# Pair 7 of the second FFN's down projection as seven block products, with a second weight sum by DMA in three groups

## The chip, the cores and the metric

The kernel runs on one core of a Trainium2 chip. The metric is the device time of one execution in microseconds: 547.79 us is the median of three runs of the kernel before. The engines are named as the profile names them: PE (TensorE), DVE (VectorE), ACT (ScalarE), POOL (GpSimd) and SP (SyncE, which issues most transfers).

## The reference

One decoder layer on 256 tokens of width 1024, all in float32: a half-step SwiGLU FFN, a mixer of two attentions, a second half-step FFN, and a final norm.

```python
def swiglu(x, w_gate, w_up, w_down):
    return (jax.nn.silu(x @ w_gate) * (x @ w_up)) @ w_down

h = h + FFN_RES * swiglu(rms_norm(h, ffn1_norm[l]), ...)
h = h + hybrid_mixer(rms_norm(h, mix_norm[l]), ...)
h = h + FFN_RES * swiglu(rms_norm(h, ffn2_norm[l]), ffn2_w_gate[l], ffn2_w_up[l], ffn2_w_down[l])
return rms_norm(h, final_norm)
```

The change is in the last product of the second FFN, the down projection: 256 x 2816 hidden values by a 2816 x 1024 matrix.

## The kernel before, in words

**Tiles and precision.** All weights come as one stream of 376 tiles of 128 x 512 floats, two to a chunk of 512 KB. A product of float32 values is made of three matmuls (`mm3`, L381 to L383): each operand is split into a high part (float32r, the rounded value) and a low part (what is left), and high x high, high x low and low x high are added in PSUM. One such triple is called a unit. For each weight tile ACT writes the high part `wh` (L236) and DVE the low part `wl` (L237); in the products that follow a norm, L240 and L241 do the same with the norm's gain. The class `Weights` does this ahead of use: 12 buffers for `wh` and `wl`, `split` at most 11 tiles ahead in the down projection, SP's loads of chunks six buffers ahead. A chunk is loaded again when the tiles in it have been read.

**The down projection.** The hidden values are 22 blocks k of 128 (11 pairs, numbered 0 to 10), by two token blocks t and two column halves c. A plain pair has 4 weight tiles, each used for both t: 8 units. In the pairs of `SEVENS` the 2 x 2 x 2 block product is made by seven units instead of eight (the Strassen-Winograd form). They use seven weight tiles, each once: tiles s, s+2, s+3 as loaded and four sums T3 to T6 of them, and four sums of the hidden blocks (`cs`, L589 to L592, then split into `c` at L412 and L413). Four results go to the banks X, Y, Z and V (`dn_f2XY`, `dn_f2ZV`), the rest directly to the outputs' banks. `post` combines X, Y, Z and V after the last such pair and adds them to the residual `h` (L710 to L724, with L707).

**Who makes the weight sums.** T3 = tile s + tile s+1 is made by GpSimd's transfers (`given`): one loads tile s (L206), a second adds tile s+1 to it in the transfer (L208). They are issued 16 and 11 places ahead of the group. T4 = tile s+3 + tile s+1, T5 = tile s+3 + T3 and T6 = tile s+2 + T5 are made by DVE (`seventh`, L216), each just before a split.

**The rest of POOL's queue.** The hidden values are transposed by 16 small transfers for each two pairs (`exchange`, L537; `hm_f<-hs_f`). For the last three pairs (8, 9 and 10) POOL issues them, between the transfers of T; then ACT and DVE split the result (`hth_f`, `htl_f`). POOL issues in order, and a transfer that adds waits for its load to land.

**The tail.** In the second FFN `TAILS` leaves the last four blocks, pairs 9 and 10, to the end: eight weight tiles, used for one output half after the other. As an output half is done, DVE adds it to `h` (`residual`, L680) and the final norm of its row block goes on: a square on ACT (L418), sums and the reciprocal root on DVE and ACT, the product with the gain (`hg`), the result and its store. The last half (1,1) comes in two pieces of 256 columns (`dn_f2p`).

**What sets the order.** From the third block of the second FFN on, all engines run in the order in which the code records instructions (`manual_schedule`). A generator-based scheduler, `Weave`, ticks once a unit; delayed steps (`post` after 3 ticks, then one step a tick) are recorded between units, and `weave.flush()` ahead of the tail records all that is left.

Of the kernel before, what the change touches and what calls it, by code (L numbers as in the profile page):

```python
# [8 lines left out]
F32 = mybir.dt.float32  # L9
# [8 lines left out]
P = 128  # L18
T = 256
# [8 lines left out]
NEG = -1e30  # L28
CH = 2
N_TILES = 376  # L30
SEVENS = (0, 2, 4, 6), (0, 2, 3, 5, 6)
ADDED = 0,
W_IN = FB * KD + 2 * KF + 3 * len(SEVENS[0])
W_BR = W_IN + 10 * KD
W_OUT = W_BR + 16
# [2 lines left out]
WB = 12  # L38
# [22 lines left out]
AHEAD0 = 4  # L61
# [42 lines left out]
class Weave:  # L104


    def __init__(self):
        self.now = 0
        self.tasks = []
# [30 lines left out]

def _items():

    out, n = [], 0

    def plain(count):
        nonlocal n
        out.extend((n + i, None) for i in range(count))
        n += count

    for f in range(2):  # L150
        plain(FB * KD)
        for g in range(KF // 2):
            if g in SEVENS[f]:
                out.extend((n, j) for j in range(7))
                n += 4
            else:
                plain(4)
        if f == 0:
            plain(W_FFN2 - W_IN)
    assert n == N_TILES  # L160
    return out


class Weights:


    def __init__(self, nc, pool, early, sums, spare, stream, gain, bufs, ahead):
        self.early, self.sums, self.spare, self.items = early, sums, spare, _items()
        self.nc, self.pool, self.stream, self.gain = nc, pool, stream, gain
        self.bufs, self.ahead = bufs, ahead  # L170
        self.loaded = self.ready = self.freed = self.at = 0
        self.raw, self.parts, self.behind = {}, {}, {}
        self.made, self.ahead_of = {}, {}
        for i, (s, j) in enumerate(self.items):
            if j == 0:
                for step, lead in enumerate((AHEAD_LOAD, AHEAD_ADD)):
                    self.ahead_of.setdefault(i - lead, []).append((s, step))

    def load(self, n, tiles=0):

        n = min(n, N_TILES // CH)
        while self.loaded < n * CH + tiles:
            c, j = divmod(self.loaded, CH)
            if j == 0:
                nm = f"raw{c}"
                self.raw[c] = self.early(nm) if c < 12 else self.pool.tile([P, CH * 512], F32, name=nm, tag="raw", bufs=RAW)
            step = 1 if c < 3 else CH
            s = slice(j * 512, (j + step) * 512)
            if {0, 1} <= set(ADDED) and (c * CH, 0) in self.items:
                s = slice(0, 512)  # L190
            for piece in HALVES if self.loaded == 0 else (s,):
                self.nc.sync.dma_start(self.raw[c][:, piece], self.stream[c, :, piece])
            self.loaded += step
# [6 lines left out]

    def given(self, s, step):

        for n in ADDED:
            if step == 0:
                self.made[s, 3 + n] = self.spare(f"T{s}_{3 + n}")
                self.nc.gpsimd.dma_start(self.made[s, 3 + n], self.source(s + 3 * n))  # L206
            else:
                self.nc.gpsimd.dma_start(self.made[s, 3 + n], self.source(s + 1), accum_op=ALU.add)  # L208

    def seventh(self, s, j):  # L210

        if 0 < j < 4 and not (j == 1 and 1 in ADDED):
            a, b, o = ((3, 1, 4), (3, 3, 5), (2, 5, 6))[j - 1]
            self.made[s, o] = self.sums(f"T{s}_{o}")
            b = self.made[s, b] if j > 1 else self.tile(s + b)
            self.nc.vector.tensor_add(self.made[s, o], self.tile(s + a), b)  # L216
        raw = self.made.pop((s, j)) if j > 2 else self.tile(s + (0, 2, 3)[j])
        return raw, {1: s // CH, 3: s // CH + 1}.get(j)
# [50 lines left out]
def hybrid_layer_kernel(ctx, tc, x, xt, pos, g_final, bgate, wstream, out):  # L269
    nc = tc.nc  # L270
# [5 lines left out]
    wpool = ctx.enter_context(tc.tile_pool(name="wpool", bufs=1))  # L276
    work = ctx.enter_context(tc.tile_pool(name="work", bufs=1))
# [11 lines left out]
    def big(nm, dt=F32R):  # L289
        return work.tile([P, 1024], dt, name=nm, tag="big", bufs=20)  # L290
# [7 lines left out]
    def row512(nm):  # L298
        return work.tile([P, 512], F32, name=nm, tag="tok", bufs=4)

    def spare512(nm):
        return work.tile([P, 768], F32, name=nm, tag="r", bufs=4)[:, 0:512]

# [6 lines left out]
    def gain(i):  # L310
# [7 lines left out]
                return gk[:, n * KD + k:n * KD + k + 1]  # L318
        return None

    W = Weights(nc, wpool, lambda nm: big(nm, F32), row512, spare512, wstream, gain, WB, AHEAD0)

    xin = [big(f"xin{j}", F32) for j in range(2)]

    def load_x(queue, k0, k1):
        s = slice(k0 % 4 * T, k0 % 4 * T + (k1 - k0) * T)
        queue.dma_start(xin[k0 // 4][:, s], xt[:, 3 * KD + k0 * T:3 * KD + k1 * T])


    nc.scalar.dma_start(first, xt[:, 0:3 * KD + T])  # L330
    W.load(0, 1)
    nc.scalar.preload_act_table_set("silu_and_others")
    W.load(1)
    load_x(nc.sync, 1, 2)
    W.load(2)
    load_x(nc.sync, 2, 3)
    W.load(3)
    load_x(nc.sync, 3, 4)
    W.load(4)
    load_x(nc.sync, 4, 6)  # L340
    W.load(6)
    load_x(nc.sync, 6, 8)
# [21 lines left out]
    sums = consts.tile([P, 2 * P], F32R, name="sums")  # L364
# [190 lines left out]
    def ffn(base, xn, nm, on_half, lag, last=False):  # L555
# [3 lines left out]
        squares = {}  # L559
        sevens = SEVENS[1 if last else 0]  # L560

# [316 lines left out]
    def project(bi, evac):  # L878
        banks = {}
        for t, k in lagged(KD, KD if bi == 0 else 2):  # L880
            if k == 0:
                banks[t] = acc_bank(f"in{bi}_{t}")
            i = W_IN + bi * KD + k
            unit(banks[t], un[t].blk(k), W.get(i), k == 0, k == KD - 1)
            if t == 1:
                W.done(i)
            if k == KD - 1:
                evac(t, banks[t])
# [219 lines left out]

    gates = {}
    for gi in range(4):  # L1110
        bg = work.tile([P, 512], F32, name=f"bg{gi}", tag="bg", bufs=2)
        src = bgate[gi * 512:(gi + 1) * 512]
        with tc.issue_after(marks["rot"]):
            nc.gpsimd.dma_start(bg, bass.AP(tensor=src.tensor, offset=src.offset, ap=[[0, P], [1, 512]]))

        def evac_g(t, ps, gi=gi, bg=bg):
            if gi % 2 == 0:
                gates[gi // 2, t] = big(f"gate{gi}_{t}", F32)
            g = gates[gi // 2, t][:, gi % 2 * 512:gi % 2 * 512 + 512]
            nc.vector.scalar_tensor_tensor(g, ps, un[t].r, bg, op0=ALU.mult, op1=ALU.add)  # L1120

        project(6 + gi, evac_g)
# [57 lines left out]
    for c in range(2):  # L1180
        s = slice(c * 512, c * 512 + 512)
# [110 lines left out]
```

## Time and profile before

| what | us |
| --- | --- |
| median of three runs (547.63, 547.79, 549.13) | 547.79 |
| the profiled execution's own time | 547.91 |
| its span, first to last instruction | 546.1 |
| PE busy / DVE busy / ACT busy / POOL busy | 538.4 / 450.1 / 355.5 / 126.2 |
| the second down projection: first weight split on ACT, last matmul's end | 473.89, 539.66 |

The span lies 1.8 us under the time of the same execution. TensorE's granted clock is 0.998 of full speed on average. A matmul's row has 0.39 us but rows start 0.227 us apart, since matmuls overlap; rows of DVE overlap by some 0.08 us in the same way. So the pace of an engine is read from starts, not from durations. In a row of the timeline the number in brackets is the engine's idle time before it, with what ended it.

### The profile page before, as it was taken

What the parts mean: (1) busy time and instruction counts of PE and PEld (TensorE: products, weight loads), DVE (VectorE), ACT (ScalarE), POOL (GpSimd) and SP (SyncE); (2) the same over time, 40 slices, a digit from 0 to 9 for tenths busy, and PEclk for the clock granted to TensorE, in tenths of its full rate; (3) what the DMA queues carried; (4) which work ended last, traced back from release to release, by engine and by line L of the source; (5) the groups of instructions that cost most, each with busy time, mean ns of one, the idle gap of its engine ahead of it and who ended that gap; (6) DMA issues with size and microseconds to landing.
All of it is one profiled execution on the core that took longest, in us unless ns stands there. A gap on an engine that the chain in (4) does not pass through costs nothing.

```text
span 546.1 us, 8019 instructions
## 1 busy us (share of the span) xinstructions
PE 538.4 (99%) x2463; PEld 444.4 (81%) x2463; DVE 450.1 (82%) x806; ACT 355.5 (65%) x616; POOL 126.2 (23%) x243
## 2 busy tenths in 40 slices
PE   9999999999999999999999999999999999999995
PEld 6888888888888888888888888888888888888884
DVE  5797799889998766889888888876667887899995
ACT  5876556658773766677876775466566566667743
POOL 2430000035405826022022220384000000157000
PEclk9999999999999999999999999999999999999999
DMA  7979766678875767446555375677656767788712
GB/s 278 405 261 307 242 210 203 208 245 269 271 239 187 240 209 217 154 155 186 174 160 175 124 243 175 192 248 224 223 180 219 224 197 240 212 277 227 233 55 77
DMA packets 44634, 116.94 MB, mean 214 GB/s; under 512 B 8640, under 2 KB 16368, under 8 KB 44592
## 3 DMA queue, kind: packets, MB, share of 16 engines
q1 hardware_dynamic: 37824, 106.82, 59.3%
q0 software_dynamic: 6480, 9.27, 6.8%
q8 instruction: 19, 0.31, 0.2%
q10 hardware_dynamic: 288, 0.36, 0.2%
q14 instruction: 23, 0.19, 0.1%
HBM read 106.97 MB, written 1.05 MB: 198 GB/s over the span
## 4 chain that ended last, share of the span: by engine, by line
PE 97%; DMA 1%; ACT 0%; SPq 0%; DVE 0%; issue 0%; ACTq 0%
PE gu_f L381 13%; PE gu_f L382 13%; PE gu_f L383 13%; PE in L381 7%; PE in L383 7%; PE in L382 7%; PE dn_f L382 5%; PE dn_f L383 5%; PE dn_f L381 5%; PE wo L381 1%; PE wo L383 1%; PE wo L382 1%; PE gu_f L394 1%; PE gu_f L395 1%; PE gu_f L397 1%; DMA raw<-in_wstream 1%
## 5 line engine op out<-in xcount | busy, mean ns | idle before, releaser
L241 DVE SCALAR_TENSOR_TENSOR wl<-raw,first,wh 128x512 fp32r<-128x512 f32 (+1 forms) x257 | 180.4, 744 | 25.4 <-ACT wh L240 25.1
L240 ACT ACTIVATE wh<-raw,first 128x512 fp32r<-128x512 f32 (+1 forms) x257 | 169.1, 714 | 23.5 <-PE in L383 7.9
L236 ACT CAST wh<-raw 128x512 fp32r<-128x512 f32 x111 | 64.3, 618 | 21.8 <-PE dn_f L383 7.3
L537 POOL DMA_DIRECT2D hm_f<-hs_f x64 | 33.9, 662 | 181.3 <-DVE wl L241 99.8
L237 DVE TENSOR_TENSOR wl<-raw,wh 128x512 fp32r<-128x512 f32 x111 | 72.7, 686 | 2.6 <-ACT wh L236 2.4
L381 PE MATMUL gu_f<-wh,zh 128*128 128x512 f32 x176 | 68.5, 389 | 0.0
L382 PE MATMUL gu_f<-wl,zh 128*128 128x512 f32 x176 | 68.5, 389 | 0.0
L383 PE MATMUL gu_f<-wh,zl 128*128 128x512 f32 x176 | 68.5, 389 | 0.0
L381 PE MATMUL in<-wh,uh 128*128 128x512 f32 x160 | 63.5, 397 | 0.0
L383 PE MATMUL in<-wh,ul 128*128 128x512 f32 x160 | 62.5, 391 | 0.0
L382 PE MATMUL in<-wl,uh 128*128 128x512 f32 x160 | 62.4, 390 | 0.0
L381 PE MATMUL gu_f<-wh,xh 128*128 128x512 f32 x144 | 56.0, 389 | 0.0
L382 PE MATMUL gu_f<-wl,xh 128*128 128x512 f32 x144 | 56.0, 389 | 0.0
L383 PE MATMUL gu_f<-wh,xl 128*128 128x512 f32 x144 | 56.0, 389 | 0.0
L381 PE MATMUL dn_f<-wh,hth_f 128*128 128x512 f32 x118 | 46.0, 390 | 0.0
L383 PE MATMUL dn_f<-wh,htl_f 128*128 128x512 f32 x118 | 45.9, 389 | 0.0
L382 PE MATMUL dn_f<-wl,hth_f 128*128 128x512 f32 x118 | 45.9, 389 | 0.0
L381 PEld LDWEIGHTS gu_f<-wh,zh 128*128 128x128 f32 x176 | 33.0, 188 | 6.9
L383 PEld LDWEIGHTS gu_f<-wh,zl 128*128 128x128 f32 x176 | 33.0, 188 | 6.9
L382 PEld LDWEIGHTS gu_f<-wl,zh 128*128 128x128 f32 x176 | 33.0, 188 | 6.7
L383 PEld LDWEIGHTS in<-wh,ul 128*128 128x128 f32 x160 | 30.0, 188 | 6.5
L381 PEld LDWEIGHTS in<-wh,uh 128*128 128x128 f32 x160 | 30.1, 188 | 6.1
(321 smaller groups left out, 974.0 us busy)
## 6 DMA issues: line engine op xcount, KB each, us to landing
raw<-in_wstream SPq DMA_DIRECT2D x185, 512.0 KB, 4.3
T<-in_wstream POOLq DMA_DIRECT2D x18, 256.0 KB, 5.1
hm_f<-hs_f SPq DMA_DIRECT2D x128, 32.0 KB, 4.0
raw<-in_wstream SPq DMA_DIRECT2D x5, 256.0 KB, 5.0
h<-in_x SPq DMA_DIRECT2D x2, 512.0 KB, 8.2
hm_f<-hs_f POOLq DMA_DIRECT2D x32, 32.0 KB, 4.7
bg<-in_bgate POOLq DMA_DIRECT2D x4, 256.0 KB, 4.6
xin<-in_xt SPq DMA_DIRECT2D x2, 256.0 KB, 6.8
```

The costliest lines, as they stand in the source:

```text
L236: self.nc.scalar.copy(hi, raw)
L237: self.nc.vector.tensor_sub(lo, raw, hi.bitcast(F32))
L240: self.nc.scalar.activation(hi[:, s], raw[:, s], AF.Copy, scale=g)
L241: self.nc.vector.scalar_tensor_tensor(lo[:, s], raw[:, s], g, hi[:, s].bitcast(F32), op0=ALU.mult, op1=ALU.subtract)
L381: nc.tensor.matmul(o, ah, wh, start=first, stop=False)
L382: nc.tensor.matmul(o, ah, wl, start=False, stop=False)
L383: nc.tensor.matmul(o, al, wh, start=False, stop=last)
L394: nc.tensor.matmul(o, ah, wh, start=first, stop=False)
L395: nc.tensor.matmul(o, al, wh, start=False, stop=False)
L397: nc.tensor.matmul(o, ah, wl, start=False, stop=last)
L537: queues[m % len(queues)].dma_start(moved[j * w:j * w + w, i * n * w:(i + 1) * n * w], squares[i * w:i * w + w, j * n * w:(j + 1) * n * w])
```

## The change

Pair 7 of the second FFN joins `SEVENS`, and in the groups of pairs 3, 6 and 7 (`BOTH`) T4 too is made by two transfers of GpSimd (tile s+3 loaded, tile s+1 added). DVE then makes only T5 and T6 there. Tile s+1 isn't needed in SBUF in these groups, so SP loads only the first half of their first chunk. T4 is put into the two buffers that held the gates' biases (tag `bg`).

```diff
-SEVENS = (0, 2, 4, 6), (0, 2, 3, 5, 6)
-ADDED = 0,
+SEVENS = (0, 2, 4, 6), (0, 2, 3, 5, 6, 7)
+BOTH = (), (3, 6, 7)
...
             if g in SEVENS[f]:
                 out.extend((n, j) for j in range(7))
+                if g in BOTH[f]:
+                    both.add(n)
                 n += 4
...
             s = slice(j * 512, (j + step) * 512)
-            if {0, 1} <= set(ADDED) and (c * CH, 0) in self.items:
+            if c * CH in self.both:
                 s = slice(0, 512)
...
-        for n in ADDED:
+        for n in (0, 1) if s in self.both else (0,):
             if step == 0:
-                self.made[s, 3 + n] = self.spare(f"T{s}_{3 + n}")
+                self.made[s, 3 + n] = self.spare[n](f"T{s}_{3 + n}")
                 self.nc.gpsimd.dma_start(self.made[s, 3 + n], self.source(s + 3 * n))
             else:
                 self.nc.gpsimd.dma_start(self.made[s, 3 + n], self.source(s + 1), accum_op=ALU.add)
...
-        if 0 < j < 4 and not (j == 1 and 1 in ADDED):
+        if 0 < j < 4 and not (j == 1 and s in self.both):
...
+    def bias512(nm):
+        return work.tile([P, 512], F32, name=nm, tag="bg", bufs=2)
+
```

Lines of the kernel after stand three further down in the class `Weights` (L216 is L219) and six further down from the second half of the diff on (L537 is L543). The order changes in the second down projection alone. Three places follow; `wl` carries the number of the weight split, `raw` that of the chunk, `T360_3` is T3 of the group that begins with tile 360 (pair 7; pair 6 is 356), and the number behind the last `_` is only a name.

DVE at pair 7, before: four low parts, then pair 8's four with the low part of the last hidden blocks between them.

```order
L237 TENSOR_TENSOR wl387_5728<-raw180_5565,wh387_5727 128x512
L237 TENSOR_TENSOR wl388_5735<-raw180_5565,wh388_5734 128x512
L237 TENSOR_TENSOR wl389_5744<-raw181_5582,wh389_5743 128x512
L237 TENSOR_TENSOR wl390_5751<-raw181_5582,wh390_5750 128x512
L237 TENSOR_TENSOR wl391_5760<-raw182_5601,wh391_5759 128x512
L237 TENSOR_TENSOR wl392_5767<-raw182_5601,wh392_5766 128x512
L413 TENSOR_TENSOR htl_f25_5774<-hm_f25_5417,hth_f25_5773 128x512
L237 TENSOR_TENSOR wl393_5778<-raw183_5622,wh393_5777 128x512
```

The same place after:

```order
L240 TENSOR_TENSOR wl387_5744<-raw180_5577,wh387_5743 128x512
L240 TENSOR_TENSOR wl388_5751<-raw181_5598,wh388_5750 128x512
L219 TENSOR_TENSOR T360_5_5759<-raw181_5598,T360_3_5583 128x512
L240 TENSOR_TENSOR wl389_5762<-raw181_5598,wh389_5761 128x512
L219 TENSOR_TENSOR T360_6_5768<-raw181_5598,T360_5_5759 128x512
L240 TENSOR_TENSOR wl390_5771<-T360_3_5583,wh390_5770 128x512
L240 TENSOR_TENSOR wl391_5780<-T360_4_5585,wh391_5779 128x512
L240 TENSOR_TENSOR wl392_5787<-T360_5_5759,wh392_5786 128x512
L419 TENSOR_TENSOR htl_f25_5794<-hm_f25_5420,hth_f25_5793 128x512
L240 TENSOR_TENSOR wl393_5798<-T360_6_5768,wh393_5797 128x512
```

Pair 7 now has seven low parts and two sums, and the low part of the last hidden blocks (`htl_f25`) stands ahead of its last weight. The four sums of pair 7's hidden blocks and their low part stand further up, among the last four weights of pair 2.

DVE at the combination of X, Y, Z and V, before:

```order
L237 TENSOR_TENSOR wl398_5821<-raw185_5701,wh398_5820 128x512
L713 TENSOR_TENSOR xy_f2_5816<-xs_f2_5815,dn_f2XY_5369 128x512
L707 SCALAR_TENSOR_TENSOR h0_71<-dn_f2XY_5369,h0_71 128x512
L237 TENSOR_TENSOR wl399_5833<-raw186_5738,wh399_5832 128x512
L715 TENSOR_TENSOR xyz_f2_5817<-dn_f2ZV_5370,xy_f2_5816 128x512
L707 SCALAR_TENSOR_TENSOR h1_72<-xyz_f2_5817,h1_72 128x512
L237 TENSOR_TENSOR wl400_5845<-raw186_5738,wh400_5844 128x512
```

The same place after:

```order
L240 TENSOR_TENSOR wl404_5875<-raw187_5774,wh404_5874 128x512
L240 TENSOR_TENSOR wl405_5890<-raw187_5774,wh405_5889 128x512
L719 TENSOR_TENSOR xy_f2_5885<-xs_f2_5884,dn_f2XY_5372 128x512
L713 SCALAR_TENSOR_TENSOR h0_71<-dn_f2XY_5372,h0_71 128x512
L721 TENSOR_TENSOR xyz_f2_5886<-dn_f2ZV_5373,xy_f2_5885 128x512
L713 SCALAR_TENSOR_TENSOR h1_72<-xyz_f2_5886,h1_72 128x512
```

Four of the last weights stood between the steps of the combination; now all eight steps follow the last weight (`wl405`) in one piece.

POOL's queue at the transfers of T for pairs 6 and 7, before:

```order
L206 DMA T356_3_5502<-in_wstream 128x512
L537 DMA hm_f24_5265<-hs_f28_5102 32x256
L537 DMA hm_f25_5417<-hs_f210_5352 32x128
L537 DMA hm_f24_5265<-hs_f28_5102 32x256
L537 DMA hm_f25_5417<-hs_f210_5352 32x128 x2
L208 DMA T356_3_5502<-in_wstream 128x512
L537 DMA hm_f25_5417<-hs_f210_5352 32x128 x7
```

The same place after, from the accumulating transfers of pair 6 on:

```order
L211 DMA T356_3_5511<-in_wstream 128x512
L211 DMA T356_4_5513<-in_wstream 128x512
L543 DMA hm_f25_5420<-hs_f210_5355 32x128
L209 DMA T360_3_5583<-in_wstream 128x512
L209 DMA T360_4_5585<-in_wstream 128x512
L543 DMA hm_f25_5420<-hs_f210_5355 32x128 x2
L211 DMA T360_3_5583<-in_wstream 128x512
L211 DMA T360_4_5585<-in_wstream 128x512
L543 DMA hm_f25_5420<-hs_f210_5355 32x128 x4
```

Pair 6 has two accumulating transfers for one, pair 7 four transfers for none, and the last four exchanges of the hidden blocks stand behind pair 7's accumulating ones.

More of the change, by code (lines that the diff above doesn't have):

```diff
@@ L141, in _items @@
 def _items():
-    out, n = [], 0
+    out, n, both = [], 0, set()
     def plain(count):
@@ L160, in _items @@
     assert n == N_TILES
-    return out
+    return out, both
 class Weights:
     def __init__(self, nc, pool, early, sums, spare, stream, gain, bufs, ahead):
-        self.early, self.sums, self.spare, self.items = early, sums, spare, _items()
+        self.early, self.sums, self.spare = early, sums, spare
+        self.items, self.both = _items()
         self.nc, self.pool, self.stream, self.gain = nc, pool, stream, gain
@@ L319, in gain @@
         return None
-    W = Weights(nc, wpool, lambda nm: big(nm, F32), row512, spare512, wstream, gain, WB, AHEAD0)
+    W = Weights(nc, wpool, lambda nm: big(nm, F32), row512, (spare512, bias512), wstream, gain, WB, AHEAD0)
     xin = [big(f"xin{j}", F32) for j in range(2)]
@@ L1110, in hybrid_layer_kernel @@
     for gi in range(4):
-        bg = work.tile([P, 512], F32, name=f"bg{gi}", tag="bg", bufs=2)
+        bg = bias512(f"bg{gi}")
         src = bgate[gi * 512:(gi + 1) * 512]
```

## The prediction

> **What bounds the kernel now.** I read the page first, then the busy time in stretches over the second down projection, then the timelines of PE, DVE, ACT and POOL there. The page gives the span, the share of each engine and the chain that ended last.
>
> ```profile
> span 546.1 us, 8019 instructions
> PE 538.4 (99%) x2463; PEld 444.4 (81%) x2463; DVE 450.1 (82%) x806; ACT 355.5 (65%) x616; POOL 126.2 (23%) x243
> PE 97%; DMA 1%; ACT 0%; SPq 0%; DVE 0%; issue 0%; ACTq 0%
> ```
>
> By these rows PE bounds the kernel and DVE has 18% to spare. But that share is a mean over stages, and the change sits in one of them. The table of stretches of 10 us (PE, weight loads, DVE, ACT, POOL, then clock, DMA share, GB/s) shows that stage.
>
> ```profile
> 470.00:480.00 10.00, 10.00 (x46) 8.29 (x45) 8.10 (x15) 6.64 (x12) 2.58 (x5) 1.00 0.79 247
> 480.00:490.00 10.00, 10.00 (x46) 8.29 (x45) 9.89 (x20) 6.77 (x12) 6.98 (x13) 1.00 0.86 265
> 490.00:500.00 10.00, 10.00 (x46) 8.29 (x45) 10.00 (x18) 6.98 (x13) 6.46 (x12) 1.00 0.88 261
> 500.00:510.00 10.00, 10.00 (x46) 8.29 (x45) 10.00 (x17) 7.29 (x13) 4.39 (x8) 1.00 0.86 260
> 510.00:520.00 10.00, 10.00 (x46) 8.29 (x45) 10.00 (x18) 8.06 (x16) 0.00 (x0) 1.00 0.57 186
> 520.00:530.00 10.00, 10.00 (x46) 8.29 (x45) 9.89 (x17) 4.53 (x8) 0.00 (x0) 1.00 0.12 46
> 530.00:540.00 10.00, 9.66 (x54) 8.29 (x53) 7.41 (x17) 3.91 (x11) 0.00 (x0) 1.00 0.14 52
> ```
>
> From 480 to 530 us DVE is as full as PE: 49.78 of 50 us. What keeps PE from waiting is a lead: the weights were split ahead of use. PE's timeline gives its pace and DVE's gives the lead.
>
> ```profile
> 517.14 0.39 PE L382 MATMUL dn_f<-wl,hth_f 128*128 128x512 f32 x1
> ...
> 517.82 0.39 PE L382 MATMUL dn_f<-wl,hth_f 128*128 128x512 f32 x1
> ...
> 539.38 0.28 PE L383 MATMUL dn_f2p<-wh,htl_f 128*128 128x256 f32 x1
> ```
>
> ```profile
> 512.99 2.49 DVE L237 TENSOR_TENSOR wl<-T,wh 128x512 fp32r<-128x512 f32 x4
> 515.40 3.70 DVE L237 TENSOR_TENSOR wl<-raw,wh 128x512 fp32r<-128x512 f32 x6
> 519.01 0.69 DVE L413 TENSOR_TENSOR htl_f<-hm_f,hth_f 128x512 fp32r<-128x512 f32 x1
> 519.61 3.70 DVE L237 TENSOR_TENSOR wl<-raw,wh 128x512 fp32r<-128x512 f32 x6
> 523.23 0.68 DVE L713 TENSOR_TENSOR xy_f<-xs_f,dn_f2XY 128x512 f32<-128x512 f32 x1
> ```
>
> A unit of three matmuls takes PE 0.68 us (517.82 less 517.14). The last low part of pair 6 is ready at 515.48 (512.99 + 2.49) and PE reads it at 517.14: the lead is down to 1.66 us just where pair 7 begins. On DVE an instruction of 512 columns follows the last after 0.603 us (519.61 to 523.23 for six). PE's last matmul ends at 539.66.
>
> **The change part by part.** *PE.* Pair 7 becomes seven units for eight: 0.68 us less, all of it on PE's chain.
>
> *DVE's additions.* Their prices are those of pair 6's sums of hidden blocks, which stand in this stretch:
>
> ```profile
> 486.24 0.28 DVE L589 TENSOR_TENSOR cs_f<-hm_f 128x128 f32<-128x128 f32 x1
> ...
> 487.17 0.68 DVE L237 TENSOR_TENSOR wl<-raw,wh 128x512 fp32r<-128x512 f32 x1
> ...
> 488.98 0.68 DVE L413 TENSOR_TENSOR c_f<-cs_f,c_f 128x512 fp32r<-128x512 f32 x1
> 489.58 0.68 DVE L216 TENSOR_TENSOR T<-raw,T 128x512 f32<-128x512 f32 x1
> ```
>
> Pair 7's four sums of blocks cost 0.93 us (486.24 to 487.17) and their low part 0.60 (488.98 to 489.58). Seven weight tiles instead of four are three more low parts, 3 x 0.603 = 1.81. Weight sums cancel: pairs 3 and 6 lose one each, pair 7 gains two, since GpSimd's transfers make the other two. DVE's total is +3.34 us. ACT gets three casts and one more, but has 2 to 3 us idle in each 10, so they are hidden. GpSimd's issues stand on POOL, idle for 3 us or more of each 10; their landings are the rival below.
>
> [...]
>
> *Does PE starve in pair 7?* Up to pair 6 DVE is later by 0.93 + 0.60 for the blocks and earlier by 2 x 0.603 for two sums: +0.33. Pair 7 then needs ten instructions before its last weight is ready (seven low parts, two sums, and the low part of the last hidden blocks, which now stands inside it): 515.48 + 0.33 + 6.03 = 521.84. PE wants it at 517.82 + 6 x 0.68 = 521.90. So the lead sinks to 0.06 us. PE loses between nothing and some 0.1 us there (the handoff between engines), and pair 8, with eight units for four weights, restores the lead.
>
> *The end.* This is the term that decides. The combination of X, Y, Z and V (eight instructions) used to run between the last four weights; it now comes behind all weights, as the order shows. DVE's work up to the first residual sums stays in one unbroken row, 3.34 us longer, while PE arrives 0.68 earlier. DVE's rows there:
>
> ```profile
> 530.81 1.28 DVE L680 SCALAR_TENSOR_TENSOR h<-dn_f,h 128x512 f32<-128x512 f32 x2
> 534.11 0.69 DVE L680 SCALAR_TENSOR_TENSOR h<-dn_f,h 128x512 f32<-128x512 f32 x1 [2.01 <-PE dn_f L383]
> 534.72 0.15 DVE L1215 TENSOR_SCALAR fin<-fin 128x1 f32<-128x1 f32 x1
> ...
> 537.26 0.69 DVE L680 SCALAR_TENSOR_TENSOR h<-dn_f,h 128x512 f32<-128x512 f32 x1
> 538.26 0.42 DVE L680 SCALAR_TENSOR_TENSOR h<-dn_f2p,h 128x256 f32<-128x256 f32 x1 [0.32 <-PE dn_f2p L383]
> 538.61 1.02 DVE L1211 TENSOR_TENSOR hg<-h,gB 128x512 f32<-128x512 f32 x2
> 539.70 0.42 DVE L680 SCALAR_TENSOR_TENSOR h<-dn_f2p,h 128x256 f32<-128x256 f32 x1
> ```
>
> DVE's whole spare time behind the weights is the 2.01 us before 534.11 (2.09, as neighbours overlap by 0.08). 3.34 - 2.09 leaves the residual of half (0,1) 1.25 us late. Then a wait that was hidden appears. ACT's square of half (0,0) must end before L1215:
>
> ```profile
> 532.13 0.63 ACT L418 ACTIVATE sq_fin<-h 128x512 bf16<-128x512 f32 x1 [6.85 <-DVE h L680]
> 532.67 0.19 ACT L418 ACTIVATION_READ_ACCUMULATOR sq_fin<-h 128x1 f32 x1
> ```
>
> It is done at 532.86, 0.77 us after the pair of residuals (532.09). With the residual of (0,1) right behind, L1215 would be ready 0.53 us after that of (0,0) ends: it now waits some 0.3 us, handoff included. 1.55 late. The wait of 0.32 (0.40) before 538.26 absorbs part: 1.15. Before 539.70 DVE waited another 0.15 (538.61 + 1.02 - 0.08 = 539.55): 1.0 us late at the last residual, from which the chain to the end is unchanged. So PE's gain is not seen, since the end no longer hangs on PE: span 546.1 + 1.0 = 547.1. The profiled execution took 547.91, so 548.9; the median of the runs shown, 547.79, is 0.12 lower: **548.8**. The terms are rows of this stage; the least sure are the overlaps, and they make it 548.3 to 549.2.
>
> **The rivals.** *A, PE's gain is kept: 547.1* (547.79 - 0.68). For it speaks the chain, 97% PE. It needs 1.7 us more slack on DVE than I count, in a stretch where no row shows idle time but the two used above. 0.07.
>
> *B, the transfers of pair 7 land late: slower.* DVE's first sum of pair 7 reads what GpSimd accumulated (T360_3), at 515.48 + 0.33 + 2 x 0.603, less the overlap: 516.9. Behind it in DVE's order stand all later weights and the whole end, so each us late is a us on the time. POOL's rows, and the time to landing of T over the whole span and from 500 to 512:
>
> ```profile
> 495.51 0.94 POOL L206 DMA_DIRECT2D T<-in_wstream  x1
> ...
> 501.14 0.93 POOL L208 DMA_DIRECT2D T<-in_wstream  x1 [2.25 <-DMA T<-in_wstream]
> 501.74 3.80 POOL L537 DMA_DIRECT2D hm_f<-hs_f  x7
> ```
>
> ```profile
> DMA to landing us min/median/max: 3.9/5.1/8.5
> ```
>
> ```profile
> DMA to landing us min/median/max: 7.3/7.3/7.3
> ```
>
> Pair 6's accumulate is issued at 501.14; behind it come its second (0.60), an exchange (0.49, seven in 3.80) and then pair 7's load: 502.8 at the earliest (0.60 for the step to the second again). Load and accumulate take 3.9 to 8.5 us each, with 0.5 between: between 511.1 and 520.3. Twice the median makes 513.5, twice the 7.3 of the busiest stretch 517.9. I take 7.3 for the load, which flies while the DMA share is 0.86, and 5.1 for the accumulate, since the share falls to 0.57: 515.7, 1.2 us early. The six transfers added, less three half chunks that SP no longer loads, push the other way. From 516.9 on B decides, and from 0.6 us later it can be measured; with 517.9 the time is 549.8, with 8.5 and 7.3 it is 551.0. The four exchanges behind the accumulates, which ACT's cast of the last hidden blocks needs, would be late with it. 0.28.
>
> The Trainium skill, "DMA: Bandwidth & Descriptors", "Anatomy of one DMA", gives 2.0 us plus bytes at 436 GB/s for such a transfer, 2.6 us for 256 KB. By that the sums land at 508.5 and B is out; no T of this trace landed that fast, so B stays.
>
> **How the numbers follow.** Forecast 0.65, A 0.07, B 0.28. A measurement of this kernel tells about 0.3% from no change, 1.64 us: below 546.15 or above 549.43. The forecast and A are within, B is above: same 0.70, slower 0.28; none of the cases is faster by that much, and 0.02 is kept for one that I do not see. The range, 547.5 to 551.0, leaves out A and the end of B.
>
> **What would show it.** Right: no idle time on DVE before the residuals of (0,1) and of piece 0; the last residual at about 540.7; PE's last matmul at about 539.0, 1.7 us before it; L1215's successor waiting for ACT. A: PE earlier by 0.68 and DVE still waiting for it at the residuals. B: DVE idle before the first sum of pair 7, released by a transfer of T, and PE idle in pair 7. Wrong altogether: DVE idle elsewhere, or a gap on PE of over 0.3 us with the transfers in time.

## The result, and the profile after

| what | before | after |
| --- | --- | --- |
| median (fastest to slowest of six runs each), us | 547.84 (547.63 to 549.13) | 553.72 (552.83 to 555.28) |
| ratio, with its 95% interval | | 1.0109 (1.009 to 1.0127) |
| the profiled execution, us | 547.91 | 553.31 |
| DVE's last residual starts, us into the span | 539.70 | 545.11 |
| PE's last matmul ends, us into the span | 539.66 | 544.78 |

The changed kernel is slower by 5.9 us, 1.1% (the interval leaves out 1), and the time lies above the range. All medians here are of runs in the chip's usual state; one run of 3115 us, of a version in experiment 5, is left out. The first lines below the title of the page of the changed kernel, and its chain by engines:

```profile
span 551.5 us, 8040 instructions
PE 541.8 (98%) x2460; PEld 445.6 (81%) x2460; DVE 453.1 (82%) x814; ACT 357.5 (65%) x620; POOL 132.4 (24%) x251
PE 91%; DVE 4%; issue 2%; DMA 1%; ACT 1%; POOL 0%; ACTq 0%; DVEq 0%; POOLq 0%
```

The span grew by 5.4 us and DVE's busy time by 3.0. The chain is the first sign: DVE has 4% of it, about 22 us, where it had nothing. The table of stretches of the changed kernel (columns as in the one of before) says where:

```profile
500.00:510.00 10.00, 10.00 (x45) 8.27 (x45) 10.00 (x17) 7.61 (x15) 5.15 (x9) 1.00 0.92 269
510.00:520.00 10.00, 9.25 (x41) 7.32 (x39) 7.21 (x13) 4.06 (x8) 3.88 (x6) 1.00 0.88 264
520.00:530.00 10.00, 8.79 (x23) 5.84 (x24) 8.60 (x15) 7.38 (x15) 0.00 (x0) 0.66 0.34 115
530.00:540.00 10.00, 10.00 (x46) 8.28 (x45) 9.79 (x17) 3.38 (x6) 0.00 (x0) 1.00 0.00 1
```

Up to 510 nothing is lost. From 510 to 530 DVE stands 4.2 us in a stretch in which it was full before, PE does 64 matmuls in 20 us in place of 92, and the clock falls to 0.66 in one slice. The transfers' share in the second row is 0.88 where it was 0.57. DVE's timeline of the changed kernel (the old L216, L237, L413 and L680 are now L219, L240, L419 and L686):

```profile
515.63 1.29 DVE L240 TENSOR_TENSOR wl<-raw,wh 128x512 fp32r<-128x512 f32 x2
519.71 0.69 DVE L219 TENSOR_TENSOR T<-raw,T 128x512 f32<-128x512 f32 x1 [2.79 <-DMA T<-in_wstream]
...
523.61 1.29 DVE L240 TENSOR_TENSOR wl<-T,wh 128x512 fp32r<-128x512 f32 x2 [1.40 <-ACT wh L239]
524.83 0.68 DVE L419 TENSOR_TENSOR htl_f<-hm_f,hth_f 128x512 fp32r<-128x512 f32 x1
...
526.03 7.31 DVE L240 TENSOR_TENSOR wl<-raw,wh 128x512 fp32r<-128x512 f32 x12
...
538.62 1.89 DVE L686 SCALAR_TENSOR_TENSOR h<-dn_f,h 128x512 f32<-128x512 f32 x3
540.69 0.15 DVE L1221 TENSOR_SCALAR fin<-fin 128x1 f32<-128x1 f32 x1 [0.19 <-ACT sq_fin L424]
...
545.11 0.42 DVE L686 SCALAR_TENSOR_TENSOR h<-dn_f2p,h 128x256 f32<-128x256 f32 x1
```

Two waits stand in pair 7, 2.79 and 1.40 us; behind them DVE's row stands nowhere longer than 0.11 us up to the residuals, as forecast. The second wait is named by ACT. ACT's own timeline shows what it waited for:

```profile
519.79 0.62 ACT L239 CAST wh<-T 128x512 fp32r<-128x512 f32 x1 [4.18 <-DMA T<-in_wstream]
522.96 1.14 ACT L239 CAST wh<-T 128x512 fp32r<-128x512 f32 x2 [2.56 <-DMA T<-in_wstream]
```

ACT casts T3 and then T4 of pair 7, and each comes late from a transfer. So both of DVE's waits are transfers of GpSimd. POOL's timeline of the changed kernel (L209 loads, L211 adds, L543 exchanges):

```profile
496.71 1.50 POOL L209 DMA_DIRECT2D T<-in_wstream  x2
...
501.02 0.95 POOL L211 DMA_DIRECT2D T<-in_wstream  x1 [0.36 <-DMA T<-in_wstream]
504.48 0.89 POOL L211 DMA_DIRECT2D T<-in_wstream  x1 [2.51 <-DMA T<-in_wstream]
505.04 0.85 POOL L543 DMA_DIRECT2D hm_f<-hs_f  x1
505.57 1.46 POOL L209 DMA_DIRECT2D T<-in_wstream  x2
506.67 1.35 POOL L543 DMA_DIRECT2D hm_f<-hs_f  x2
513.89 1.85 POOL L211 DMA_DIRECT2D T<-in_wstream  x2 [5.87 <-DMA T<-in_wstream]
```

The third row holds what I had not counted: pair 6's second adding transfer waits 2.51 us for its own load, and pair 7's loads stand behind it in the queue. They go out at 505.57. The three lines below give the times to landing in the changed kernel, of pair 6's two loads, of pair 7's two loads and of pair 7's two adding transfers:

```profile
DMA to landing us min/median/max: 4.0/5.5/6.9
...
DMA to landing us min/median/max: 8.0/8.1/8.2
...
DMA to landing us min/median/max: 5.8/7.0/8.2
```

The first sum lands at 513.89 + 5.8 = 519.7, where DVE wanted it at 516.9; the second, issued 0.74 later, takes 8.2 and lands at 522.9.

PE's timeline shows the stall and what follows it:

```profile
518.86 0.39 PE L387 MATMUL dn_f<-wh,c_f 128*128 128x512 f32 x1
521.06 0.50 PE L388 MATMUL dn_f<-wl,c_f 128*128 128x512 f32 x1 [1.81 <-DVE wl L240]
...
527.08 0.63 PE L388 MATMUL dn_f<-wl,hth_f 128*128 128x512 f32 x1
527.51 0.63 PE L389 MATMUL dn_f<-wh,htl_f 128*128 128x512 f32 x1
```

After the gap of 1.81 us matmuls start 0.43 us apart (527.08 to 527.51) in place of 0.227. The trace has the granted clock at 0.5 from 521.46 to 528.29. Whether the transfers, the half clock or DVE's added work make the 5.4 us is what the experiments tell apart.

### The profile page after: what moved, and what is told of

Same layout as the page of the kernel before. It is cut to its first block, busy times and chain, and to the rows that moved or that the text cites. A ratio compares the mean times of both kernels' runs of the same rounds, so it can differ in the third digit from the quotient of the medians.

```text
span 551.5 us, 8040 instructions
## 1 busy us (share of the span) xinstructions
PE 541.8 (98%) x2460; PEld 445.6 (81%) x2460; DVE 453.1 (82%) x814; ACT 357.5 (65%) x620; POOL 132.4 (24%) x251
## 4 chain that ended last, share of the span: by engine, by line
PE 91%; DVE 4%; issue 2%; DMA 1%; ACT 1%; POOL 0%; ACTq 0%; DVEq 0%; POOLq 0%
PE gu_f L387 13%; PE gu_f L389 13%; PE gu_f L388 13%; PE in L387 7%; PE in L389 7%; PE in L388 7%; PE dn_f L389 4%; PE dn_f L388 4%; PE dn_f L387 3%; DVE wl L240 2%; PE wo L387 1%; PE wo L389 1%; PE wo L388 1%; PE gu_f L400 1%; PE gu_f L401 1%
## 5 line engine op out<-in xcount | busy, mean ns | idle before, releaser
L543 POOL DMA_DIRECT2D hm_f<-hs_f x64 | 35.4, 681 | 182.4 <-DVE wl L244 99.8
L240 DVE TENSOR_TENSOR wl<-raw,wh 128x512 fp32r<-128x512 f32 x110 | 71.6, 684 | 2.7 <-ACT wh L239 2.4
L387 PE MATMUL dn_f<-wh,hth_f 128*128 128x512 f32 x112 | 44.1, 394 | 0.0
L389 PE MATMUL dn_f<-wh,htl_f 128*128 128x512 f32 x112 | 43.8, 391 | 0.0
L388 PE MATMUL dn_f<-wl,hth_f 128*128 128x512 f32 x112 | 43.8, 391 | 0.0
L239 ACT CAST wh<-T 128x512 fp32r<-128x512 f32 x40 | 24.3, 620 | 21.9 <-DVE T L219 11.8
```

What stands on the lines that cost most here:

```text
L239: self.nc.scalar.copy(hi, raw)
L240: self.nc.vector.tensor_sub(lo, raw, hi.bitcast(F32))
L387: nc.tensor.matmul(o, ah, wh, start=first, stop=False)
L388: nc.tensor.matmul(o, ah, wl, start=False, stop=False)
L389: nc.tensor.matmul(o, al, wh, start=False, stop=last)
L543: queues[m % len(queues)].dma_start(moved[j * w:j * w + w, i * n * w:(i + 1) * n * w], squares[i * w:i * w + w, j * n * w:(j + 1) * n * w])
```

## The experiments

All ratios are to the kernel before, run on the same chip, with 95% intervals. "Last residual" is the start of DVE's last L686 row (L680 in before, 539.70); "PE's end" the end of the last matmul (539.66 in before).

**1. Pair 7 by seven, without transfers.** DVE makes T3 and T4 of pair 7 itself.

```diff
-BOTH = (), (3, 6, 7)
+BOTH = (), (3, 6)
+NONE = 360
...
-        for n in (0, 1) if s in self.both else (0,):
+        for n in (0, 1) if s in self.both else () if s == NONE else (0,):
...
+        if j == 1 and s == NONE:
+            self.made[s, 3] = self.spare[0](f"T{s}_3")
+            self.nc.vector.tensor_add(self.made[s, 3], self.tile(s), self.tile(s + 1))
```

> Pair 7 stays seven products, but both its first weight sums (T3 and T4) are made by DVE and none by transfers; pairs 3 and 6 as in the changed kernel. Theory (the changed kernel is 1.0 us late by DVE's added work, and 4.2 us more by DVE standing still for pair 7's transfers): two sums more on DVE, 2 x 0.60, and no wait for transfers, so 547.84 + 1.0 + 1.2 = 550.0, with the last residual 2.2 us behind that of the kernel before. Rival 1 (PE's gap and the half clock after it are the cost, DVE's work isn't): no long gap, so PE's gain less about 1.1 us of starving, 548.3. Rival 2 (the added transfers as a load on the DMA engines): four of six are gone, about 549.

550.29 us, 1.0045 (1.003 to 1.006): 3.4 us faster than the change, with two more sums on DVE. The last residual starts at 542.24, 2.54 later than before: the forecast's 1.0, two more sums (1.21) and one wait of 0.26 for pair 6's T4. No clock drop. So without pair 7's transfers the work of the change costs what was forecast for it, and these transfers cost more than the sums that they save. Both rivals (548.3 and 549) lie below the interval.

**2. The same transfers earlier.** Pair 7's loads are issued 22 places ahead and its adding transfers 16 (16 and 11 in the change), into buffers of their own, so that they need not wait for pair 6's sums to be read.

```diff
-                for step, lead in enumerate((AHEAD_LOAD, AHEAD_ADD)):
+                for step, lead in enumerate((22, 16) if s == 360 else (AHEAD_LOAD, AHEAD_ADD)):
...
-                self.made[s, 3 + n] = self.spare[n](f"T{s}_{3 + n}")
+                self.made[s, 3 + n] = self.spare[2 if s == 360 else n](f"T{s}_{3 + n}")
...
-    W = Weights(nc, wpool, lambda nm: big(nm, F32), row512, (spare512, bias512), wstream, gain, WB, AHEAD0)
+    W = Weights(nc, wpool, lambda nm: big(nm, F32), row512, (spare512, bias512, lambda nm: wide(nm, 512)), wstream, gain, WB, AHEAD0)
```

> The changed kernel with pair 7's four transfers issued earlier: 22 and 16 places ahead of the group instead of 16 and 11, so that its loads stand in POOL's queue ahead of pair 6's accumulating transfers; its two sums are put into other free buffers, since those of the changed kernel are not free yet. Same work everywhere. Theory: no wait of DVE in pair 7, only the 1.0 us of added work is left: 548.9. Rival 2 (the load of six more transfers, wherever they stand in the queue): stays above 552. Rival 1 (half clock): about 547.2 if PE's path alone counted, since there is no gap.

549.39 us, 1.003 (1.0019 to 1.0041): the same bytes and the same work, 4.3 us faster. DVE's timeline of this version, with one short wait for pair 6's T4 and none for pair 7:

```profile
514.25 1.89 DVE L240 TENSOR_TENSOR wl<-T,wh 128x512 fp32r<-128x512 f32 x3 [0.49 <-ACT wh L239]
...
517.26 0.68 DVE L219 TENSOR_TENSOR T<-raw,T 128x512 f32<-128x512 f32 x1
...
541.15 0.41 DVE L686 SCALAR_TENSOR_TENSOR h<-dn_f2p,h 128x256 f32<-128x256 f32 x1
```

The last residual is 1.45 later than before: 0.57 for that wait (0.49 and the overlap of two rows) and 0.9 for the rest, where the forecast said 1.0. That wait is also why the time is 0.5 above the 548.9 expected. With the same transfers in time neither rival is left (552 or more; 547.2), and the lateness is shown as the cause of the 4.3 us.

**3. The transfers of the other pairs alone.** Pair 7 stays plain, pairs 3 and 6 keep the second transfer.

```diff
-SEVENS = (0, 2, 4, 6), (0, 2, 3, 5, 6, 7)
-BOTH = (), (3, 6, 7)
+SEVENS = (0, 2, 4, 6), (0, 2, 3, 5, 6)
+BOTH = (), (3, 6)
```

> Pair 7 as eight products again, the second sum by transfers kept for pairs 3 and 6: only the transfers' part of the change. Theory: DVE has 1.2 us less work, PE is the bound as before and nothing waits: 547.8, no change within 0.3%. Rival 2: four transfers of the six and the longer queue cost: 549 or more.

547.86 us, 1.0001 (0.9992 to 1.001). DVE waits for PE again (2.03 us before the residual of half (0,1)). Sums by transfer cost nothing where they are in time, and bring nothing while PE sets the end.

**4. PE kept busy.** The change with 16 matmuls of zeros, ten behind pair 7's second unit and six behind its V unit. They add nothing to the sums.

```diff
+                if last and g == 7 and o in ((0, 0), "V"):
+                    bank = common["V"] if o == "V" else out_bank(*o)
+                    fill = 6 if o == "V" else 10
+                    for f in range(fill):
+                        nc.tensor.matmul(bank.rearrange("p (a b) -> p a b", b=P), zeros,
+                                         zeros.unsqueeze(1).to_broadcast([P, 4, P]), start=False, stop=o == "V" and f == fill - 1)
```

> The changed kernel with 16 matmuls of zeros added to banks in pair 7 (ten behind the second unit, six behind the fourth), where PE stands still: they add nothing to the values and keep PE busy. Theory: DVE's wait for the transfers is as long as before and DVE's row sets the end, so the time stays, 553.5 within 0.8, with PE's clock full and PE's last matmul some 2 us earlier than without. Rival 1 (half clock): the clock stays up and the time falls by 2 us or more, to 551.5 or below.

553.7 us, 1.0108 (1.0091 to 1.0125). The table of stretches and DVE's timeline of this version:

```profile
520.00:530.00 10.00, 9.52 (x41) 6.36 (x40) 7.88 (x14) 7.03 (x14) 0.00 (x0) 1.00 0.36 118
```

```profile
518.87 0.69 DVE L219 TENSOR_TENSOR T<-raw,T 128x512 f32<-128x512 f32 x1 [1.61 <-DMA T<-in_wstream]
...
523.46 1.29 DVE L240 TENSOR_TENSOR wl<-T,wh 128x512 fp32r<-128x512 f32 x2 [2.10 <-ACT wh L239]
```

The clock is 1.00 where it was 0.66 and PE's end comes at 543.37, 1.4 earlier (some 2 were expected). DVE's two waits are still there (1.61 + 2.10); with 0.43 for pair 6's T4 ahead of them they are 4.14 us, against 4.19 in the change. The last residual (545.06) and the time do not move. So the half clock is real and costs nothing here: DVE's standing sets the end.

**5. GpSimd as DVE's helper.** The remaining loss in experiment 2 is DVE's row at the end, and POOL is idle there. I took it that GpSimd could make some low parts and free DVE. Seven versions use this one edit, with different tiles:

```diff
-            self.nc.vector.tensor_sub(lo, raw, hi.bitcast(F32))
+            (self.nc.gpsimd if i >= len(self.items) - 4 else self.nc.vector).tensor_sub(lo, raw, hi.bitcast(F32))
```

On the kernel before (the last four tiles):

> Control: the kernel before with the low parts of the last four weights made by GpSimd. Theory: PE bounds it, DVE's 2.4 us less buys nothing, 547.8. Rival (GpSimd's share is itself the gain): 547.2 or less; or GpSimd is too slow for the tail and PE waits: above 548.5.

547.78 us, 0.9999 (0.999 to 1.0008), as expected. On the change, the last four:

> The changed kernel, its late transfers kept, with the low parts of the last four weights made by GpSimd. DVE's row ends 2.4 us earlier. Theory: the late transfers hold up both DVE and PE; PE's last matmul ended only 0.3 us before the last residual, with its gap and its half clock, so PE takes over as the bound and the time falls by 0.3 to 0.6 us only: 553.2. Rival (only DVE's row counts): 551.4.

553.25 us (median of four runs, 551.68 to 553.9), 1.009 (1.0075 to 1.0106). The interval holds the 553.2 of the theory and not the 551.4 of the rival, but it overlaps that of the change without GpSimd's help (1.009 to 1.0127), so a gain is not shown, and no timeline tells what set the end. On experiment 2 with pair 6's transfers earlier too (20 and 13 places, pair 7's 24 and 18), the last four:

> The changed kernel with the transfers of pairs 6 and 7 issued earlier (20 and 13, 24 and 18 places ahead) and the low parts of the last four weights made by GpSimd (free by then) instead of DVE. Theory: DVE has 2.4 us less at the end and no wait, so its row no longer sets the end; PE's gain of one unit appears: 547.84 - 0.68 = 547.2, the last residual waits for PE again. Rival (DVE's added work isn't what costs the 1.0 us): 548.9, as with the early transfers alone.

549.51 us, 1.003 (1.0018 to 1.0041): missed, nothing gained on experiment 2. On experiment 1, the last six:

> Both first weight sums of pair 7 by DVE, none of its weights by transfers, and the low parts of the last six weights by GpSimd. Theory: DVE's end is 3.6 us earlier than in the run without GpSimd's share and no longer counts; what is left is PE starving in pair 7, as its lead of 0.06 us is short by the two sums, 1.2 us: 547.2 + 1.2 = 548.3. Rival (pair 7's starving costs nothing by itself): 547.2.

550.44 us, 1.0046 (1.0033 to 1.006): missed too. DVE waits for PE again, but PE now waits for GpSimd, 0.61 and 0.27 us in the tail. DVE's and POOL's timelines of the run on experiment 2 with the last four tiles show why the help does not come:

```profile
528.43 0.69 DVE L719 TENSOR_TENSOR xy_f<-xs_f,dn_f2XY 128x512 f32<-128x512 f32 x1 [0.61 <-ACT xs_f L716]
...
529.64 0.68 DVE L721 TENSOR_TENSOR xyz_f<-dn_f2ZV,xy_f 128x512 f32<-128x512 f32 x1
530.35 1.66 DVE L713 SCALAR_TENSOR_TENSOR h<-xyz_f,h 128x512 f32<-128x512 f32 x1
531.94 0.68 DVE L723 TENSOR_TENSOR xyv_f<-dn_f2ZV,xy_f 128x512 f32<-128x512 f32 x1
532.65 1.07 DVE L713 SCALAR_TENSOR_TENSOR h<-xyv_f,h 128x512 f32<-128x512 f32 x1
```

```profile
526.97 6.20 POOL L240 TENSOR_TENSOR wl<-raw,wh 128x512 fp32r<-128x512 f32 x4 [10.40 <-ACT wh L239]
```

While GpSimd subtracts (526.97 to 533.17), DVE's instructions with two inputs in SBUF (`h<-xyz_f,h`) take 1.66 and 1.07 us in place of 0.69, and those that read one input from PSUM (`dn_f2ZV`) still take 0.68. That costs 1.35 us of the 2.4 that DVE saves, and the first row's wait for ACT's copy of X another 0.61. A low part has both inputs in SBUF, on either engine. Three more versions put GpSimd's tiles where DVE itself makes low parts. On experiment 2, tiles 387, 388, 389, 395 and 397:

> Pair 7's transfers early (22 and 16 places ahead), and five low parts made by GpSimd at a place where DVE runs only plain subtractions and sums and GpSimd's queue is empty: the first three of pair 7 and two of pair 8. Theory: DVE has 3.0 us less work, no longer sets the end and no longer starves PE in pair 7; what is left of the change is PE's 0.68 us: 547.85 - 0.68 = 547.2, PE's last matmul at about 539.0 and DVE waiting for it. Rival (GpSimd's subtractions slow DVE down wherever they stand, or come too late for PE): 548.5 or more.

553.65 us, 1.0106 (1.0091 to 1.0121). On experiment 2, tiles 387 to 389:

> As the run with five, but only the first three low parts of pair 7 by GpSimd: DVE 1.8 us less than with the early transfers alone, whose last residual was 1.45 us behind that of the kernel before. Theory (DVE's row sets the end): 549.4 - 1.8 = 547.6, between PE's bound (547.2) and the kernel before. Rival: 548.5 or more.

551.57 us, 1.0067 (1.005 to 1.0083). On the change, tiles 395, 397, 399, 401 and 403:

> The changed kernel with its late transfers, five low parts of pair 8 and the tail by GpSimd, after the wait for the transfers: DVE's row ends 3.0 us earlier. Theory: the late transfers stop PE as well (a gap of 1.8 us and then half clock), and its last matmul came only 0.3 us ahead of the last residual, so PE takes over: 553.2. Rival (only DVE's row counts): 550.7.

555.82 us, 1.014 (1.0125 to 1.0156). All three missed by 2.6 to 6.5 us; in the first two the rival's 548.5 or more came, in the third neither. DVE's and POOL's timelines of the first of them, in pair 7:

```profile
516.17 3.48 DVE L219 TENSOR_TENSOR T<-raw,T 128x512 f32<-128x512 f32 x2
519.57 2.96 DVE L240 TENSOR_TENSOR wl<-T,wh 128x512 fp32r<-128x512 f32 x3
522.45 1.78 DVE L419 TENSOR_TENSOR htl_f<-hm_f,hth_f 128x512 fp32r<-128x512 f32 x1
524.16 1.76 DVE L240 TENSOR_TENSOR wl<-T,wh 128x512 fp32r<-128x512 f32 x1
```

```profile
515.97 4.81 POOL L240 TENSOR_TENSOR wl<-raw,wh 128x512 fp32r<-128x512 f32 x3 [1.10 <-ACT wh L239]
522.28 3.08 POOL L240 TENSOR_TENSOR wl<-raw,wh 128x512 fp32r<-128x512 f32 x2 [1.50 <-ACT wh L239]
```

While GpSimd subtracts (1.6 us each, 4.81 for three) DVE's instructions take 1.7 to 1.8 each (3.48 for two, 1.78, 1.76), so DVE, with fewer low parts to make, has pair 7's last one ready at 525.9 (the fourth row, 524.16 + 1.76), against 522.2 in experiment 2, and PE waits for both engines. My theory that GpSimd frees DVE fell. The Trainium skill, "SBUF — State Buffer", "Who interferes with whom", has the reason: a DVE instruction with two SBUF inputs gets its second one through the read interface that it shares with GpSimd, and one with at most one SBUF input does not contend. The rows agree, 1.66 and 1.07 against 0.68. I had not weighed it before the runs.

**6. DVE's row shortened.** Experiment 2 with the last two steps of the combination left out (four DVE instructions).

```diff
-            for step in (
+            steps = (
...
+            for step in steps[:4] if last else steps:
...
+            if last:
+                return
```

> The version with pair 7's transfers early, with the last two steps of the combination left out (V plus the sum of X and Y, its residual of half (0,1), V plus the sum of all, its residual of half (1,1)): four DVE instructions of 512 columns, 4 x 0.603 = 2.41 us less in DVE's row at the end, so the output lacks V's share in those two halves. That version measured 549.39, its last residual at 541.15 and PE's last matmul at 539.46. My theory (with the transfers in time DVE's unbroken row behind the last weight sets the end, and hides PE's shorter work): DVE now waits for PE again before the last residuals, which come at 539.5, and the time is 547.6, 1.8 under that version; PE's end stays at 539.5, as 0.49 of its 0.68 us of gain is lost to the wait for pair 6's second sum. Rival (the end of that version hangs on something else than DVE's amount of work, so DVE's row in the combination is beside the point): 549.4, or less than 0.7 us under it.

547.99 us, 1.0005 (0.9996 to 1.0014): 1.4 us under experiment 2, where 1.8 was expected and the rival said at most 0.7. DVE's timeline of this version, and PE's row in pair 7:

```profile
534.23 0.69 DVE L686 SCALAR_TENSOR_TENSOR h<-dn_f,h 128x512 f32<-128x512 f32 x1 [0.76 <-PE dn_f L389]
...
539.82 0.42 DVE L686 SCALAR_TENSOR_TENSOR h<-dn_f2p,h 128x256 f32<-128x256 f32 x1
```

```profile
520.17 0.50 PE L388 MATMUL dn_f2ZV<-wl,c_f 128*128 128x512 f32 x1 [0.24 <-DVE wl L240]
```

DVE waits for PE again and the last residual is at 539.82, as before. So with the transfers in time DVE's row at the end sets the time, as forecast. PE's end is at 539.78 (539.5 expected), not earlier than before: its gain of 0.68 is gone in pair 7, where it waits for low parts. In this version DVE also waited 0.58 us for pair 6's T3, which it did not in experiment 2.

The steps from the change back to before: 553.7 to 549.4 by the transfers in time, 549.4 to 548.0 by 2.41 us of DVE's work less; the 0.2 left is inside the interval. No version tried beats the kernel before.

## Why the prediction was wrong

*What bounds the kernel*: right. DVE full from 480 to 530 is why a late transfer went straight into the time.

*DVE's additions and the end*: right. The row behind the last weight stands nowhere longer than 0.11 us, L1221 waits 0.19 for ACT (0.3 forecast), and with the transfers in time the last residual is 0.9 later beside the wait for pair 6's T4 (1.0 forecast). In the change itself, 5.41 less 2.79 and 1.40 and two overlaps of 0.08 leaves 1.06. The wait for pair 6's T4, 0.57 us with the transfers early, is in no term: that sum too comes by the added transfers, and its landing was not worked out.

*PE in pair 7*: the forecast loss was 0 to 0.1. With the transfers early, four steps of PE there are longer, as in these rows of experiment 2 (steps of 0.41, 0.34, 0.45 and 0.34 for 0.23, so 0.6 us):

```profile
519.39 0.39 PE L387 MATMUL dn_f2ZV<-wh,c_f 128*128 128x512 f32 x1
519.80 0.50 PE L388 MATMUL dn_f2ZV<-wl,c_f 128*128 128x512 f32 x1
520.14 0.39 PE L389 MATMUL dn_f2ZV<-wh,c_f 128*128 128x512 f32 x1
...
521.76 0.40 PE L387 MATMUL dn_f<-wh,hth_f 128*128 128x512 f32 x1
522.21 0.50 PE L388 MATMUL dn_f<-wl,hth_f 128*128 128x512 f32 x1
522.55 0.40 PE L389 MATMUL dn_f<-wh,htl_f 128*128 128x512 f32 x1
```

A lead of 0.06 us was no lead: the 0.57 that DVE stands at 514.25 uses it up. Rival A would not have come with more slack at DVE's end alone: in experiment 6 DVE has 2.41 us less there and PE still ends at 539.78.

*The step that failed* is the landing of pair 7's first sum, "515.7, 1.2 us early", in rival B, and with it B's chance and the forecast. It landed at 519.7, 4.0 later, by four terms. The loads were put at "502.8 at the earliest" and went out at 505.57: +2.8, since I let pair 6's second adding transfer follow the first after 0.60, and it waited 2.51 for its load. The load took 8.0 for 7.3: +0.7. The step between was 0.3 for 0.5: -0.2. The adding transfer took 5.8 for 5.1: +0.7, with the transfers' share from 510 to 520 at 0.88 and not at the 0.57 of before. In that stretch the trace has 0.97 MB moved for GpSimd, none before, and 1.67 MB for SP in place of 1.84. The 7.3 that I gave to the load was an adding transfer's; the 5.1 that I gave to the adding transfer was the median of loads and adding transfers over the whole span. From 516.9 the price was as forecast, a us for a us (2.79). What no term held is the second sum, T360_4, 3.2 us behind the first (8.2 to landing): another 1.40. B's upper end of 551.0 had two slow transfers, but neither the wait in the queue nor the second sum. With both waits and their overlaps the forecast span of 547.1 becomes 547.1 + 2.79 + 1.40 + 0.16 = 551.45; it was 551.5.

The sign was there to be read: the row of before that I quoted for the 501.14 has the adding transfer waiting 2.25 us for its load. I took it as a time stamp. A second pair of transfers in the same queue adds a wait of that kind (0.36 and 2.51 us in the change), and a forecast that hung on 1.2 us between 511.1 and 520.3 could not give B 0.28 and itself 0.65.

The time to landing of all transfers of T in the changed kernel:

```profile
DMA to landing us min/median/max: 3.8/5.8/8.2
```

The Trainium skill's 2.6 us ("DMA: Bandwidth & Descriptors", "Anatomy of one DMA") would have had the sums in time; no T landed that fast, and the ones that mattered took 5.8 to 8.2. The measurement decides.

## What to carry to other kernels

In a queue that issues in order, every transfer that waits for an earlier one (here: add after load) holds back all behind it; when a change adds such pairs, walk through the queue row by row with each wait of its own, and land the last of them, not the first. Where the engine that reads the result is already full to the end of the program, its wait is the kernel's loss one for one, and issuing the same transfers earlier is the first thing to try. Before work is moved to an idle engine, look at whether it reads memory the same way as the busy one: the idle time on a profile's page is no promise of help.

## What the runs showed of the hardware beyond that

- DVE beside GpSimd: 512 columns with two SBUF inputs take 1.06 to 1.8 us while GpSimd subtracts, 0.68 otherwise; with one input in PSUM they stay at 0.68.
- PE's clock fell to half for 6.8 us after one gap of 1.81 us. In the version with five tiles of pairs 7 and 8 on GpSimd it fell for 3.4 us after a gap of 2.12 us, so the longer gap had the shorter drop; in the one with tiles 387 to 389, gaps of 0.62 and 0.71 us did not do it.
- An adding transfer issued earlier does not land earlier by as much. In experiment 2 issuing pair 7's two adding transfers 8 us sooner brought their landing forward by 4.6 and 5.1 us. Their times to landing, with that of pair 6's second one (8.7):

```profile
DMA to landing us min/median/max: 8.7/9.2/11.2
```
